# Up projection of a hybrid DiT layer: operands from fp32r pairs to scaled fp16 pairs, sizes from a second read of the weights, and a new order of products

## The chip, the core and the metric

The kernel runs on one core of a Trainium2 chip. The metric is device time in microseconds of one execution; the median of three runs is given.

## The reference

One layer of a diffusion transformer over 1024 latent tokens of width 1024 with 256 context tokens: a modulated RMS norm, one input projection that feeds a bidirectional chunkwise mLSTM and a windowed attention, two branch projections with sigmoid gates, an output projection, and a convolutional feed-forward part. The change touches the feed-forward part, cut to this:

```
x = x_mid + g2[:, None, :] * conv_ffn(modulate(rms_norm(x_mid, norm2_w[l]), sh2, sc2),
                                      w_up[l], conv_w[l], conv_b[l], w_down[l])

def conv_ffn(h, w_up, conv_w, conv_b, w_down):
    u = h @ w_up                                  # (1024, 1024) @ (1024, 5632)
    up = jnp.pad(u, ((0, 0), (r, r), (0, 0)))
    acc = conv_b
    for j in range(CONV_W):                       # width 3 along the tokens
        acc = acc + up[:, j:j + L] * conv_w[j]
    a, g = jnp.split(acc, 2, axis=-1)
    return (jax.nn.silu(g) * a) @ w_down
```

## The kernel before, in words

Products are kept near fp32 accuracy by splitting each operand into a high and a low half and adding three products (high x high, high x low, low x high): `product` (line 2021) issues three matmuls for each of four blocks of the inner dimension, each a 128x128 weight tile against 512 columns. `split_from` (line 50) makes the halves: ACT copies the high half (line 47), DVE subtracts it from the source for the low half (line 54; with a scale, line 56). Before the change the halves of the feed-forward part are fp32r, four bytes each; in the input projection they are fp16.

The tail (`stage_tail`) runs in stages. *Branch products* (960 to 1113 us): `branch("a")` and then `branch("m")`, seven products each by a Strassen-Winograd scheme, operand by operand from a queue (`operands`, i from 0 to 13 in each branch); sigmoid gates load on the ACT queue (line 1760). *Output projection* (1113 to 1208 us): `project` in two halves; then rows are normed (`square`, lines 1869 to 1874, with GpSimd's power), transposed and split into the activations' seven operands (`put`): b11, b21, t1 to t4, b22. *Unit stage* (1208 to 1645 us): the up projection in 22 units. A unit is one pair of 128 columns of `w_up` for the value half and the gate half, and again a Strassen-Winograd scheme: seven products with weight operands r1 (two products), q1 (two), q2 (two) and r2 (one), 7 x 4 x 3 = 84 matmuls. `lead` loads a unit's megabyte of weights on the SP queue and splits r1; `prep` and `prep2` make sums of the weight quarters (s12, s34) and split q1, q2, r2. `first_mm` runs the b11 product into bank pa and the b21 product into bank pc, `first_ev` empties them into the tile ua, `rest` does the other five into pa and pb, with an eviction (ACT copy or DVE addition) after each. `conv_gate` applies the convolution (one ACT operation, two DVE ones of three operands, for each half), the silu, the gate's product, and stores the result. In the same units DVE also makes sums of the down projection's weights (`weight_sums`), and later of the hidden rows (`hidden_sums`). *Down projection* (1645 us to the end): seven products again; while it runs, the last modulation rows (`last_row`, lines 2306 and 2308; tiles u4) are summed on DVE, and `mod_row` (line 288) adds each over the partitions by small fp32 matmuls.

A scheduler orders each engine's instructions from this program order. Each engine runs its own list in order, and an instruction waits for its operands and for its output's buffer. Pools hand out tiles: `x512` pools 0 to 6 hold eight tiles of 128x512 f32 each, `op4` ten of 128x1024, `op2` four of 128x512, `raw` two megabyte tiles, `accp` eight of 128x1024.

Of the kernel before, what the change touches and what calls it, by code (L numbers as in the profile page):

```python
# [18 lines left out]
P = 128  # L19
# [1583 lines left out]
def stage_tail(E, st):  # L1603
# [52 lines left out]

    g1b = tp1.tile([P, D], F32, name="g1b")
# [91 lines left out]

    def branch(nm, sg_d, pool):  # L1750
# [85 lines left out]
    def norm_factors():  # L1836

        nc.vector.scalar_tensor_tensor(m2[:, 1], m2[:, 1], 1.0, vecT[:, V_N2 : V_N2 + KT], op0=ALU.add, op1=ALU.mult)
        nc.vector.tensor_scalar(m2[:, 1], m2[:, 1], float(D) ** 0.5, None, op0=ALU.mult)

    sM.close()

# [7 lines left out]
    xj = tp1.tile([P, 640], F32, name="xj")[:, :512]  # L1850
# [33 lines left out]
    def put(m, k, src, s=slice(0, 512)):  # L1884
        if B.setdefault(m, [None] * H)[k] is None:
            B[m][k] = [x512(f"{m}{x}{k}", pool=homes[m]) for x in "hl"]
# [50 lines left out]
    def weight_sums(k, a0, a1, b0, b1, eng=None):  # L1937
# [11 lines left out]
        nc, lambda j: A["w_up"][j], lambda n: rawp.tile([P, KT, 256], F32, tag="raw", name=n), op4, op2,  # L1949
# [14 lines left out]
    norm_factors()  # L1964
    with tc.issue_after(held.ins):
# [18 lines left out]
    U.prep_apart(0, lambda n, dt=F32R: x512(n, dt, 1))  # L1984
# [34 lines left out]
    E.__dict__.update(xm_d=xm_d, g2b=g2b, T=T, weight_sums=weight_sums, sA=sA, sX=sX, x512=x512, rawp=rawp, op4=op4, op2=op2, accp=accp, U=U)  # L2019
# [12 lines left out]
class Units:  # L2032
# [3 lines left out]
    def __init__(self, nc, src, raw, op4, op2, bank, out, B):  # L2036
        self.nc, self.src, self.raw, self.op4, self.op2, self.bank, self.out, self.B = nc, src, raw, op4, op2, bank, out, B
# [15 lines left out]
    def lead(self, j):  # L2053
        self.raws[j] = raw = self.raw(f"ur{j}")
        self.nc.sync.dma_start(raw, self.src(j))
        if j != 2:
            self.R1[j] = self.pair(j, "r1", self.op4, raw[:, :, 0:P])

    def lead_first(self, j):
# [3 lines left out]
        self.R1[j] = self.pair(j, "r1", self.op4, raw)  # L2063
# [20 lines left out]
    def prep(self, j):  # L2084
# [6 lines left out]
        self.Q[j] = [self.pair(j, "q1", self.op4, s12)]  # L2091

    def prep2(self, j):
# [5 lines left out]
        self.Q[j] += [self.pair(j, "q2", self.op4, s34), self.pair(j, "r2", self.op2, a22)]  # L2099

    def prep_apart(self, j, new):
# [3 lines left out]
        s1, s2, s3, s4 = [self.v(new(f"s{i}_{j}", F32)) for i in range(1, 5)]  # L2105
# [4 lines left out]
        self.Q[j] = [sum([self.pair(j, f"q1{i}", new, s) for i, s in enumerate((s1, s2))], [])]  # L2110
# [338 lines left out]
```

## Time and profile before

| | |
|---|---|
| median of 3 runs | 1845.76 us (1845.05 to 1845.76) |
| profiled execution | 1849.14 us, span 1847.4 us |
| branch products | 960 to 1113 us |
| output projection, transposes | 1113 to 1208 us |
| unit stage | 1208 to 1645 us |
| down projection | 1645 to 1847 us |
| one unit in the middle | 19.04 us |

A row of the timeline reads: start, duration, engine, line, operation, out <- in by the program's names, shape. Matmuls are pipelined, so the pace of TensorE is read from start to start and not from durations; the same holds for the busy times of DVE and ACT, whose operations overlap by about 0.1 us. A row of windows gives the busy time and the number of instructions of each engine, the granted clock of TensorE, the share of the DMA engines and GB/s. `x8` on an fp32 matmul counts the passes that were recorded together.

### The profile page before, as it was taken

To read this page: it belongs to the slowest core of one execution; us is meant where nothing else is said; L and a number is where in the kernel's file an instruction comes from. 1 tells how busy PE (TensorE), PEld (TensorE's weight loads), DVE (VectorE), ACT (ScalarE), POOL (GpSimd) and SP (SyncE) were. 2 spreads that over 40 slices of the span, in tenths; PEclk is the share of its full clock that TensorE was granted. 3 is DMA by queue.
4 is the path that set the end of the run, shared out by engine and by line. 5 is a ranking of instruction groups with operands and counts; after the bars stand their busy time and mean duration, and the time that the engine had idled before them with its cause. 6 is when DMAs were issued, how large, how long until landed. Compare 5 with 4: busy or idle time off the path is not lost.

```text
span 1847.4 us, 27864 instructions
## 1 busy us (share of the span) xinstructions
PE 1790.8 (97%) x9207; PEld 1283.5 (69%) x9207; DVE 1425.9 (77%) x2864; ACT 1069.8 (58%) x2229; POOL 508.3 (28%) x747
## 2 busy tenths in 40 slices
PE   7989999999998899999999999999999999999999
PEld 3855555555554566656668887878888888888887
DVE  3858888888788686858687787698889898897665
ACT  4747877878787565645356462476444444465441
POOL 2467769587862530303010020000000000000000
PEclk9999999999999899999999999999999999999999
DMA  9747988888796625261359927322454544599751
GB/s 342 233 138 146 201 170 179 192 180 199 147 182 131 219 79 192 79 213 37 132 188 368 344 92 246 141 77 106 172 207 180 194 160 166 195 318 371 260 172 69
DMA packets 302193, 342.47 MB, mean 185 GB/s; under 512 B 176208, under 2 KB 200672, under 8 KB 299232
## 3 DMA queue, kind: packets, MB, share of 16 engines
q1 hardware_dynamic: 287648, 314.47, 56.3%
q10 hardware_dynamic: 14400, 26.22, 4.2%
q8 instruction: 72, 1.18, 0.3%
q14 instruction: 73, 0.60, 0.1%
HBM read 224.61 MB, written 76.16 MB: 163 GB/s over the span
## 4 chain that ended last, share of the span: by engine, by line
PE 78%; DVE 7%; DMA 4%; issue 3%; ACT 3%; POOL 3%; SPq 0%; ACTq 0%; DVEq 0%; POOLq 0%
PE g L706 8%; PE pq L706 6%; PE pa L2027 4%; PE pa L2029 4%; PE pa L2028 4%; PE po L706 3%; PE dx L2029 2%; PE dx L2027 2%; PE dx L2028 2%; PE pb L2027 2%; PE pb L2029 2%; PE pb L2028 2%; PE yb L2029 2%; PE yb L2027 2%; PE yb L2028 2%
## 5 line engine op out<-in xcount | busy, mean ns | idle before, releaser
L850 DVE CUSTOM_DVE_ANT_0 s<-s,maskA,nsink 128x640 f32<-128x640 f32 (+1 forms) x128 | 117.4, 917 | 65.5 <-PE s L845 65.0
L866 DVE TENSOR_TENSOR P<-s,P 128x640 f16<-128x640 f32 (+1 forms) x128 | 100.6, 786 | 1.0 <-ACT s L861 1.0
L860 ACT ACTIVATE P<-s,st 128x640 f16<-128x640 f32 (+1 forms) x128 | 98.2, 767 | 4.1
L706 PE MATMUL g<-hH,fh 128*128 128x512 f16 x256 | 97.1, 379 | 0.0
L706 PE MATMUL g<-hH,fl 128*128 128x512 f16 x256 | 97.0, 379 | 0.0
L706 PE MATMUL g<-hL,fh 128*128 128x512 f16 x256 | 97.0, 379 | 0.0
L861 ACT ACTIVATE s<-s,st 128x640 f32<-128x640 f32 (+1 forms) x128 | 93.8, 733 | 0.0
L706 PEld LDWEIGHTS <-hH 128*128 128x128 f16 x640 | 62.8, 99 | 37.3 <-issue 1.8
L858 ACT ACTIVATE st<-st,shift 128x1 f32<-128x1 f32 x128 | 37.6, 294 | 85.6 <-DVE st L850 84.8
L706 PE MATMUL pq<-wha,hH 128*128 128x384 f16 (+1 forms) x256 | 84.9, 332 | 0.1
L706 PE MATMUL pq<-wha,hL 128*128 128x384 f16 (+1 forms) x256 | 84.9, 332 | 0.0
L706 PE MATMUL pq<-wla,hH 128*128 128x384 f16 (+1 forms) x256 | 84.9, 332 | 0.0
L706 PEld LDWEIGHTS <-fh 128*128 128x128 f16 x512 | 49.2, 100 | 45.4
L2165 ACT ACTIVATE cv<-ua,vecT 128x1024 f32<-128x1024 f32 x22 | 27.4, 1246 | 84.9 <-DVE ua L2138 84.9
L1436 POOL TENSOR_SCALAR kwh<-k,gcall 128x128 fp32r<-128x128 f32 x72 | 32.5, 455 | 157.2 <-PE dC L164 53.9
L47 ACT ACTIVATE dfh<-drf 128x512 fp32r<-128x512 f32 x55 | 34.4, 628 | 59.3 <-PE dx L2028 26.5
L2027 PE MATMUL dx<-dwh,dfh 128*128 128x512 f32 (+1 forms) x176 | 68.3, 388 | 0.0
L2029 PE MATMUL dx<-dwh,dfl 128*128 128x512 f32 (+1 forms) x176 | 68.2, 388 | 0.0
L2028 PE MATMUL dx<-dwl,dfh 128*128 128x512 f32 (+1 forms) x176 | 68.2, 387 | 0.0
L54 DVE TENSOR_TENSOR dfl<-drf,dfh 128x512 fp32r<-128x512 f32 x55 | 37.6, 688 | 36.1 <-ACT dfh L47 36.1
L165 PE MATMUL kv<-whkv,hL 128*128 128x384 f16 x192 | 62.6, 326 | 0.0
L164 PE MATMUL kv<-wlkv,hH 128*128 128x384 f16 x192 | 62.6, 326 | 0.0
(691 smaller groups left out, 6249.9 us busy)
## 6 DMA issues: line engine op xcount, KB each, us to landing
ur<-in_w_up SPq DMA_DIRECT2D x22, 1024.0 KB
wmb<-in_w_modB SPq DMA_DIRECT2D x48, 256.0 KB
f_d<-cv SPq DMA_DIRECT2D x22, 512.0 KB
wm<-in_w_modA SPq DMA_DIRECT2D x16, 512.0 KB
fr<-in_w_g SPq DMA_DIRECT2D x32, 256.0 KB
drf<-fs_d SPq DMA_DIRECT2D x15, 512.0 KB
drw<-wt_d SPq DMA_DIRECT2D x14, 512.0 KB
w1b<-in_w_cx SPq DMA_DIRECT2D x16, 388.0 KB
```

The source lines that it names most:

```text
L54: rest = nc.vector.tensor_tensor(lo, src, whole, op=ALU.subtract)
L164: nc.tensor.matmul(ps, lh[:, ls], rl[:, rs], start=False, stop=False)
L165: nc.tensor.matmul(ps, ll[:, ls], rh[:, rs], start=False, stop=stop and i == n - 1)
L706: nc.tensor.matmul(self.ps, x, w, start=self.i == 0, stop=self.i == self.n - 1)
L850: nc.vector.tensor_tensor_reduce(e, e, self.mask, scale=self.ss[:, h : h + 1], scalar=nsink[:, hh : hh + 1], op0=ALU.add, op1=ALU.min, acc ...
L858: nc.scalar.activation(m, st4[:, 8 + h : 9 + h], AF.Identity, bias=shift)
L860: nc.scalar.activation(two[:, :W], e, AF.Exp, bias=m, scale=-1.0)
L861: nc.scalar.activation(e, e, AF.Exp, bias=m, scale=-1.0, accum_out=st4[:, 4 + h : 5 + h])
L866: nc.vector.tensor_tensor(two[:, W : 2 * W], self.e[h], two[:, :W], op=ALU.subtract)
L2027: nc.tensor.matmul(ps, lh, rh, start=start and i == 0, stop=False, skip_group_check=True)
L2028: nc.tensor.matmul(ps, lh, rl, start=False, stop=False, skip_group_check=True)
L2029: nc.tensor.matmul(ps, ll, rh, start=False, stop=stop and i == n - 1, skip_group_check=True)
```

## The change

Four things change together.

1. Every operand of the up projection is an fp16 pair: high and low half lie in one tile of the size of one former half. The weights are multiplied by a factor of their unit as they are split, so the split's DVE part becomes a three-operand instruction. The activations are scaled by one factor (`xbound`), worked into the norm's scale and shift.
2. A unit's factor is a power of the sum of the squares of its weights. The weights are read a second time for it, in four pieces of 256 KB (`size_load`): for units 0 to 3 on the ACT queue during the branch products, for the others on the SP queue four units ahead. ACT squares each piece with a sum along the row (`measure`); `measured` adds the four columns over the partitions by four fp32 matmuls with a matrix of ones (bank ub), then one DVE operation, a power on GpSimd, a reciprocal on DVE, and two GpSimd operations that put the inverse factors into the convolution's weights.
3. From unit 2 on, the next unit's first two products stand inside a unit: b11 between t1 and t3, b21 between b22 and t4. `prep` and `prep2` of the next unit are issued inside the unit, the sizes of the third unit ahead are added up just before t4, and r1 is split two units ahead.
4. The weights of a unit are fetched one unit earlier (`fetch(j + 3)`).

```diff
+    def measure(j, i, raw):
+        if i == 0:
+            F[j] = tp1.tile([P, 16], F32, tag="uf", name=f"uf{j}", bufs=8)
+        w = E.junk[:, : raw.shape[1]] if raw.shape[1] <= E.junk.shape[1] else raw
+        nc.scalar.activation(w, raw, AF.Square, accum_out=F[j][:, i : i + 1])
+    def size_load(pool, j, k, queue):
+        um = pool(f"um{j}{k}")
+        queue.dma_start(um.rearrange("p (k c) -> p k c", k=2), A["w_up"][j][:, 2 * k : 2 * k + 2])
+        UM.append((j, k, um))
+    def ahead_sizes(n):
+        if 6 <= n < 22:
+            size_load(lambda nm: up.tile([P, 512], F32, tag="um", name=nm), (n - 6) // 4, (n - 6) % 4, nc.scalar)
+        if 8 <= n < 24:
+            measure(*UM.pop(0))
...
             for i in (2 * p, 2 * p + 1):
+                ahead_sizes(i if nm == "a" else 14 + i)
...
+        q = tp1.tile([P, 24], F32, name="xbound")
+        nc.gpsimd.tensor_tensor(q[:, 8:16], m2[:, 1], m2[:, 1], op=ALU.mult)
+        nc.scalar.activation(q[:, 16:24], q[:, 8:16], AF.Square, accum_out=q[:, 0:1])
+        nc.scalar.activation(q[:, 16:24], m2[:, 0], AF.Square, accum_out=q[:, 1:2])
+        nc.tensor.matmul(pb[:, 0:2], E.ones, q[:, 0:2], start=True, stop=True)
...
+        nc.gpsimd.tensor_scalar(m2, m2, xs_[:, 0:1], None, op0=ALU.mult)
+    def measured(j, n):
+        f = F[j]
+        pb = tp_tile(f"ub{j}")
+        for i in range(n):
+            nc.tensor.matmul(pb[:, 0:1], E.ones, f[:, i : i + 1], start=i == 0, stop=i == n - 1)
+        nc.vector.tensor_scalar(f[:, 4:5], pb[:, 0:1], 2.0 ** -26, 1e-36, op0=ALU.mult, op1=ALU.add)
+        nc.gpsimd.tensor_tensor(f[:, 5:6], f[:, 4:5], expo[:, 0:1], op=ALU.pow)
+        nc.vector.reciprocal(f[:, 6:7], f[:, 5:6])
+        nc.gpsimd.tensor_scalar(f[:, 7:8], f[:, 6:7], xs_[:, 1:2], None, op0=ALU.mult)
+        nc.gpsimd.tensor_scalar(f[:, 8:14].rearrange("p (i u) -> p i u", i=3), cw, f[:, 7:8], None, op0=ALU.mult)
...
     def pair(self, j, nm, new, src):
-        p = self.v(new(f"{nm}h{j}")), self.v(new(f"{nm}l{j}"))
-        split_from(self.nc, *p, src)
+        p = [self.v(t) for t in new(f"{nm}{j}")]
+        split_from(self.nc, *p, src, scale=self.F[j][:, 5:6])
...
         product(nc, pb, op(q1, 0), B["t1"], True)
         copy_act(nc, ug[:, t1], pb)
+        between(0)
+        if new is not None:
+            r1 = self.R1.pop(new)
+            na, un = self.bank("A", f"pa{new}"), self.out("u", f"ua{new}")
+            product(nc, na, self.op(r1, 0), B["b11"], True)
+            copy_act(nc, un[:, t0], na)
         product(nc, pa, op(q2, 0), B["t3"], False)
         nc.vector.tensor_tensor(ug[:, t1], pa, ug[:, t1], op=ALU.add)
+        between(1)
         product(nc, pb, op(q2, 4), B["b22"], False)
         nc.vector.tensor_tensor(ua[:, t1], pb, ua[:, t1], op=ALU.add)
+        if new is not None:
+            pc = self.bank("C", f"pc{new}")
+            product(nc, pc, self.op(r1, 4), B["b21"], True)
+            nc.vector.tensor_tensor(un[:, t0], pc, un[:, t0], op=ALU.add)
+            self.mid[new] = na, un
+        between(2)
         product(nc, pa, op(r2, 0), B["t4"], False)
...
+    def between(j):
+        def part(i):
+            n = j + 2
+            if 2 <= j < NFC - 1 and i < 2:
+                (U.prep, U.prep2)[i](j + 1)
+            if 4 <= n + 1 < NFC and i == 2:
+                E.measured(n + 1, 4)
+        return part
...
+        elif j + 2 < NFC:
+            U.lead(j + 2)
+        if 1 <= j < NFC - 3:
+            U.fetch(j + 3)
+        if 4 <= j + 4 < NFC:
+            for k in range(4):
+                E.size_load(lambda nm: E.x512(nm, F32, 4), j + 4, k, nc.sync)
         sums(j - 1, a)
         a = conv_gate(j, *u)
+        while E.UM:
+            E.measure(*E.UM.pop(0))
```

How the order of instructions moves is shown at three places. First TensorE before, at the end of unit 14 and the start of unit 15 (pa14 is the unit's bank, t4h and t4l the halves of the activations' operand, r2 and r1 the weights'):

```order
L2027 MATMUL pa14_16660<-t4h3_14757,r2h14_16636 128x512
L2028 MATMUL pa14_16660<-t4l3_14758,r2h14_16636 128x512
L2029 MATMUL pa14_16660<-t4h3_14757,r2l14_16637 128x512
L2027 MATMUL pa15_16800<-b11h0_14285,r1h15_16758 128x512
L2028 MATMUL pa15_16800<-b11l0_14286,r1h15_16758 128x512
L2029 MATMUL pa15_16800<-b11h0_14285,r1l15_16759 128x512
```

After, the same engine just ahead of unit 14's t4 (both halves now bear one name; ub17 is the bank of unit 17's sizes, uf17 its columns):

```order
L2095 MATMUL pc15_17114<-b213_14510,r115_16992 128x512
L2096 LDWEIGHTS r115_16992
L2096 MATMUL pc15_17114<-b213_14510,r115_16992 128x512
L2097 LDWEIGHTS r115_16992
L2097 MATMUL pc15_17114<-b213_14510,r115_16992 128x512
L1897 MATMUL ub17_17128<-uf17_17025,ones_106 128x1 x4
L2095 LDWEIGHTS r214_16939
L2095 MATMUL pa14_16905<-t40_14825,r214_16939 128x512
```

The next unit's b21 product (pc15) and the four sizing matmuls of unit 17 now stand ahead of unit 14's t4, and weight loads are instructions of their own.

Second VectorE in the same unit, before (cv are the convolution's tiles, q1l, q2l and r1l the low halves):

```order
L2167 SCALAR_TENSOR_TENSOR cv14_36_16793<-ug14_16690,vecT_68,cv14_36_16793 128x1023
L2077 TENSOR_TENSOR ua15_16826<-pc15_16801,ua15_16826 128x512
L54 TENSOR_TENSOR q1l16_16906<-s12_16_16902,q1h16_16905 128x1024
L2171 TENSOR_TENSOR cv14_14_16789<-cv14_14_16789,cv14_36_16793 128x1024
L2097 TENSOR_TENSOR s34_16_16909<-ur16_16896 128x512
```

and after:

```order
L2250 SCALAR_TENSOR_TENSOR cv14_14_17173<-ua14_16906,uf14_16543,cv14_14_17173 128x1023
L2219 TENSOR_TENSOR ua15_17065<-pc15_17114,ua15_17065 128x512
L1898 TENSOR_SCALAR uf17_17025<-ub17_17128 128x1
L2251 SCALAR_TENSOR_TENSOR cv14_14_17173<-ua14_16906,uf14_16543,cv14_14_17173 128x1023
L1900 RECIPROCAL uf17_17025<-uf17_17025 128x1
L2162 TENSOR_TENSOR s12_17_17376<-ur17_17154 128x512
L56 SCALAR_TENSOR_TENSOR r117_17310<-ur17_17154,uf17_17025,r117_17310 128x1024
```

The size's two one-column operations stand between the eviction and the sums, with one convolution operation between them, and the splits take the factor uf17 as a third operand.

Third ScalarE at the start of the branch products, before (baw and baa are the weights and the activations of branch a):

```order
L47 ACTIVATE bawh1_0_12181<-bawr1_12179 128x512
L47 ACTIVATE baah2_0_12227<-baar2_12225 128x512
L47 ACTIVATE bawh1_1_12183<-bawr1_12179 128x512
L47 ACTIVATE baah3_0_12279<-baar3_12277 128x512
L47 ACTIVATE baah2_1_12229<-baar2_12225 128x512
L47 ACTIVATE baah1_0_12201<-baar1_12199 128x512
```

and after (um01 is the second piece of unit 0's sizes, xj a scratch tile):

```order
L47 ACTIVATE bawh1_0_12181<-bawr1_12179 128x512
L47 ACTIVATE baah2_0_12231<-baar2_12229 128x512
L1772 ACTIVATE xj_12220,uf0_12673<-um00_12555 128x512
L47 ACTIVATE bawh1_1_12183<-bawr1_12179 128x512
L47 ACTIVATE baah2_1_12233<-baar2_12229 128x512
L47 ACTIVATE baah1_0_12201<-baar1_12199 128x512
L47 ACTIVATE bawh2_0_12241<-bawr2_12239 128x512
L47 ACTIVATE baah1_1_12203<-baar1_12199 128x512
L47 ACTIVATE baah3_0_12283<-baar3_12281 128x512
L1772 ACTIVATE xj_12220,uf0_12673<-um01_12621 128x512
L1778 DMA um10_12794<-in_w_up 128x512
L1772 ACTIVATE xj_12220,uf0_12673<-um02_12671 128x512
```

The square of unit 0's first piece now stands behind the first two splits of the branch, and two more squares and an issue of a load behind the next six.

Two things move without being named in the diff. Eight of the sixteen `last_row` sums (tiles u4_0 and their loads) stand in the unit stage, since the tiles of x512 pool 3 are free earlier. Six squares of units 5 and 6 (um50 to um61) stand on ACT ahead of the q11 split of unit 1.

More of the change, by code (lines that the diff above doesn't have):

```diff
@@ L1885, in put @@
         if B.setdefault(m, [None] * H)[k] is None:
-            B[m][k] = [x512(f"{m}{x}{k}", pool=homes[m]) for x in "hl"]
+            B[m][k] = xpair(f"{m}{k}", homes[m])
         split_from(nc, *[o[:, s] for o in B[m][k]], src)
@@ L1964, in stage_tail @@
     norm_factors()
+    for j in range(4):
+        measured(j, 4)
     with tc.issue_after(held.ins):
@@ L2018, in stage_tail @@
         put("t4", k, raw0(k + H))
-    E.__dict__.update(xm_d=xm_d, g2b=g2b, T=T, weight_sums=weight_sums, sA=sA, sX=sX, x512=x512, rawp=rawp, op4=op4, op2=op2, accp=accp, U=U)
+    E.__dict__.update(xm_d=xm_d, g2b=g2b, T=T, weight_sums=weight_sums, sA=sA, sX=sX, x512=x512, rawp=rawp, op4=op4, op2=op2, accp=accp, U=U, measure=measure, measured=measured, size_load=size_load, UM=UM)
     stage_ffn(E, st)
```

90 lines of the change are left out of this document (58 added, 32 removed).

## The prediction

> **What bounds the kernel now.** I read the page first: its busy line, then the chain that ended last.
>
> ```profile
> span 1847.4 us, 27864 instructions
> PE 1790.8 (97%) x9207; PEld 1283.5 (69%) x9207; DVE 1425.9 (77%) x2864; ACT 1069.8 (58%) x2229; POOL 508.3 (28%) x747
> PE 78%; DVE 7%; DMA 4%; issue 3%; ACT 3%; POOL 3%; SPq 0%; ACTq 0%; DVEq 0%; POOLq 0%
> ```
>
> TensorE sets the time; the other engines matter where they make it wait. Second, the windows, for the stages that the change touches (columns: busy time and instructions of PE, PEld, DVE, ACT, POOL; granted clock; DMA share; GB/s).
>
> ```profile
> 960.00:990.00 30.00, 29.07 (x127) 23.32 (x126) 23.23 (x39) 15.59 (x30) 0.00 (x0) 1.00 1.01 378
> 990.00:1020.00 30.00, 30.00 (x134) 24.86 (x133) 25.59 (x43) 22.24 (x42) 0.00 (x0) 1.00 1.01 359
> 1050.00:1080.00 30.00, 30.00 (x134) 24.86 (x133) 24.62 (x37) 19.91 (x38) 5.77 (x4) 1.00 0.57 193
> 1208.00:1300.73 92.73, 91.11 (x406) 74.12 (x405) 86.34 (x133) 58.38 (x96) 2.47 (x1) 1.00 0.26 91
> 1300.73:1319.77 19.04, 19.04 (x85) 15.77 (x84) 16.89 (x20) 9.03 (x12) 0.00 (x0) 1.00 0.51 193
> 1605.37:1624.41 19.04, 19.04 (x85) 15.77 (x84) 16.05 (x21) 11.37 (x19) 0.00 (x0) 1.00 0.91 330
> ```
>
> The last two rows are one unit of the up projection each: 84 matmuls in 19.04 us, no gap, full clock. So a unit is 84 x 226.7 ns and nothing else, and DVE has 2.15 us to spare in it, ACT 10. The front of the stage (1208 to 1300.7) is tighter: PE idles only 1.62 us there, but DVE is busy 93%. The branch products, where the first sizes are now loaded, have DMA engines that are full until 1050 and yet no PE gap after 990.
>
> **The change part by part.** *fp16 halves.* The number of matmuls stays; each takes the pace of an fp16 stream. Here are the first and the last of 48 fp16 matmuls of that shape (timeline of TensorE):
>
> ```profile
> 944.60 0.39 PE L163 MATMUL mo<-hH,whqo 128*128 128x512 f16 x1
> 954.75 0.38 PE L165 MATMUL mo<-hH,wlqo 128*128 128x512 f16 x1
> ```
>
> 10.15 us / 47 = 216 ns, against 19.04 / 84 = 226.7. Saved: 10.7 ns x 84 = 0.90 us per unit, x 22 = **-19.7 us**, as far as TensorE stays the bound.
>
> *Sizing matmuls.* Each unit gets four fp32 matmuls of a 128x128 matrix of ones against one column. The kernel has this form already, in the row products of the modulation (an fp16 neighbourhood first, then the down projection's f32 one):
>
> ```profile
> 323.64 0.95 PE L288 MATMUL ms<-expo,macc 128*128 128x1 f32 x8
> 324.45 0.32 PE L842 MATMUL s<-KA,QT 128*128 128x384 f16 x1
> ...
> 1713.72 0.95 PE L288 MATMUL dy<-expo,u 128*128 128x1 f32 x8
> 1714.53 0.49 PE L2027 MATMUL dx<-dwh,dfh 128*128 128x512 f32 x1
> 1714.86 0.39 PE L2028 MATMUL dx<-dwl,dfh 128*128 128x512 f32 x1
> ```
>
> Four matmuls are eight passes and hold the stream 0.81 us; behind them the f32 neighbour needs 0.33 to the next start instead of 0.227, so 0.91 there. They stand inside the stream, just ahead of t4, and nothing can run beside them on PE. Eighteen units x 0.81 = 14.6; the four of units 0 to 3 stand in the f32 output projection: 4 x 0.91 = 3.6; the two-column product of the activations' scale about 0.3 (an estimate, a third of that). **+18.5 us.** The upper bound is 0.91 for all, +20.3; the lower is the case in which short passes hide under the long stream, 0, and I know no row that shows it. A unit becomes 84 x 0.216 + 0.81 = 18.95 us. The page "FP8 and Floating Point Precision" of the Trainium skill (section TensorE Precision Notes) says that a true fp32 product takes four passes through the array; by it the block would be sixteen passes and twice as long. The row shows x8 for four matmuls, so the trace does not agree, and I keep 0.81.
>
> *DVE in a unit.* It gives its time by pitch, start to start (timeline of VectorE):
>
> ```profile
> 1311.90 1.28 DVE L2166 SCALAR_TENSOR_TENSOR cv<-ug,vecT,cv 128x1023 f32<-128x1023 f32 x1
> 1313.09 0.69 DVE L1906 TENSOR_TENSOR wb<-wb 128x512 f32<-128x512 f32 x1
> 1313.70 1.28 DVE L2167 SCALAR_TENSOR_TENSOR cv<-ug,vecT,cv 128x1023 f32<-128x1023 f32 x1
> 1314.89 0.69 DVE L2077 TENSOR_TENSOR ua<-pc,ua 128x512 f32<-128x512 f32 x1
> 1315.49 1.22 DVE L54 TENSOR_TENSOR q1l<-s,q1h 128x1024 fp32r<-128x1024 f32 x1
> 1316.62 1.22 DVE L2171 TENSOR_TENSOR cv<-cv,cv 128x1024 f32<-128x1024 f32 x1
> ```
>
> 1.19 for the three-operand form, 0.60 and 1.13 for two operands. Before: 4 x 1.19 + 12 x 0.60 + 4 x 1.13 = 16.5. The scaled splits are three-operand (+0.06 on each of three long ones and on the short one: +0.24), and the two one-column operations add about 0.25: 17.0. New waits: the reciprocal stands one long operation behind the sum it needs, with GpSimd's power in between. That power has a normal and a bad size:
>
> ```profile
> 1211.69 2.47 POOL L1874 TENSOR_TENSOR rrx<-rrx,expo 128x1 f32<-128x1 f32 x1 [7.88 <-DVE rrx L1873]
> L1874 POOL TENSOR_TENSOR rrx<-rrx,expo 128x1 f32<-128x1 f32 x8 | 6.3, 792 | 93.6 <-DVE rrx L1873 93.6
> ```
>
> (6.3 - 2.47) / 7 = 0.55 us in seven cases, 2.47 in the one that ran beside two-operand work of DVE. I take about 1 us of waiting per unit, so DVE needs 18 of 18.95: **0**, and it is the thinnest cover of the change. The moved products leave evictions more room, since pa and pb are now written again after 24 matmuls (24 x 0.216 = 5.2 us) instead of 12.
>
> *ACT.* Squares cost, by pitch (timeline of ScalarE):
>
> ```profile
> 1210.18 0.63 ACT L1870 ACTIVATE xj<-acc 128x512 f32<-128x512 f32 x1 [0.59 <-DVE acc L1861]
> 1210.72 0.19 ACT L1870 ACTIVATION_READ_ACCUMULATOR xj<-acc 128x1 f32 x1
> 1210.82 0.40 ACT L47 ACTIVATE t1h<-acc 128x256 fp32r<-128x256 f32 x1
> ```
>
> 0.64 each, four per unit = 2.6 us; ACT goes from 9.0 to 11.6 of 18.95. Hidden: **0** in the steady units.
>
> *The second read.* 22 MB. In a steady unit the measured 193 GB/s has room for one more MB (+55). Four MB fall into the branch products, mostly while the DMA engines are full: 3 MB / 370 GB/s is 8 us of transfer at worst. PE shows 30.00 of 30 there, and the share falls to 0.57 after 1050, so operands lead by enough; between 0 and +8, I take **+0.5**. SP's queue passes, per unit, a fetch one unit earlier and four small loads; their buffers are free a unit ahead, and the stores behind them have no reader within the unit: 0.
>
> *Start of the branch products.* Here ACT feeds PE directly, and the measures of unit 0 stand between its splits (order of ScalarE).
>
> ```profile
> 959.54 0.50 PE L2027 MATMUL yb<-baah,bawh 128*128 128x512 f32 x1 [2.48 <-ACT bawh L47]
> 960.73 0.50 PE L2027 MATMUL yb<-baah,bawh 128*128 128x512 f32 x1 [0.46 <-DVE mo L1534]
> 962.60 0.96 PE L2029 MATMUL yb<-baah,bawl 128*128 128x512 f32 x3 [0.47 <-DVE bawl L54]
> 958.51 0.33 ACTq L1760 DMA_DIRECT2D sga<-sga_d  x1
> ```
>
> One measure stands ahead of all but the first two splits, two issues of sizes (0.33 each) and three more measures follow. The first product is paced by ACT for some 4 us; one measure is 0.64, all four and two issues 3.2. Between 0.6 and 3.2: **+1**. If a measure's load is late, ACT waits with all splits behind it (rival C).
>
> *Front of the units.* DVE is 93% busy, and here it gets the scale and size operations, the scaled splits, the waits on GpSimd, and 8 rows of the modulation sum that the order moves forward out of the down projection, since their buffers come free earlier:
>
> ```profile
> L2308 DVE SCALAR_TENSOR_TENSOR u<-u,sil,u 128x512 f32<-128x512 f32 x14 | 10.5, 747 | 2.0 <-DMA u<-in_w_modB 2.0
> ```
>
> 8 x 0.75 = 6.0 for the rows and 3 x 1.5 for the first three units (0.5 of work and 1.0 of waits, as above), 10.5 in all. PE wants 3 x 0.9 = 2.7 less there and DVE had 92.73 - 86.34 = 6.4 of idle time: upper bound 10.5 + 2.7 - 6.4 = +6.8. Lower bound -1.6, PE's idle time there. Some of the rows stand in later units with spare time, so **+2**, nearer to the lower end.
>
> Sum: -19.7 + 18.5 + 0.5 + 1 + 2 = +2.3. The profiled execution takes 1849.14 (its span and 1.74), which is 3.38 above the median of the runs; it would be 1851.4, and the median 1845.76 + 2.3 = **1848.0**.
>
> **The rivals.**
> *A. The sizes are cheap.* If the short passes hide, the 18.5 goes: 1829.5; at half of their price 1838.8. For it: PE's weight loads are overlapped everywhere else. Against it: both rows of L288 show the full 0.81. The same side is reached, just, if every stall lies at its low end: -1.2 net of PE (-19.7 + 18.5), -1.6 in the front and about -1 of the waits at the branch's start give 1842. Together 0.18.
> *B. DVE becomes the bound of a unit.* Place: the reciprocal between the two convolution operations, and GpSimd's two scalings behind it. Price: a power of 2.47 leaves 2.47 - 1.19 = 1.3 us of wait, the two scalings beside three-operand work may hold DVE about 0.5 each: 17.0 + 1.3 + 1.0 = 19.3, with a wait for the split's high half (0.2) 19.5; 18 units x 0.55 = +10, so 1858. It decides from the point at which DVE's unit passes 18.95. The page "SBUF — State Buffer" (section Who interferes with whom) states that a DVE instruction with two SBUF inputs contends with a GpSimd instruction that reads SBUF; the row of 2.47 agrees, and whether DVE too is held no row shows. Chance 0.15.
> *C. ACT waits in order for sizes.* Place: the first splits of branch a, and the q11 split of unit 1, which stands behind six measures whose buffers the measures before them free. Price: one round trip of a transfer at its worst row below, 4.8, once or twice less the cover of two units: +4 to +8, 1852 to 1856. Chance 0.2.
>
> ```profile
> 1210.17 4.77 DMA xm_d<-acc
> ```
>
> *D. The pace does not come,* because fp16 weights are loaded by instructions of their own. Then +19.7 and 1868. Against it: the quoted fp16 products load weights the same way. Chance 0.02.
>
> **How the numbers follow.** The forecast has 0.45; A 0.18, B, C and D 0.37. About 0.2%, 3.7 us, is what a measurement of this kernel can tell from no change; the forecast's own range is taken as that band, 1842.1 to 1849.4. Leaving out D, half of A and the far end of B, the range is 1841 to 1858. Faster 0.18, same 0.45, slower 0.37.
>
> **What would show it.** In the profile after: matmuls of pa and pb at 216 ns; a block of x8 on ub holding PE 0.81 us; steady units of 18.95 us with no other gap; a branch start about 1 us longer. The forecast is wrong if a unit is 18.3 or less (A), if PE waits for DVE in steady units (B), or if ACT idles on a size load while PE waits for a split (C).

## The result and the profile after

The changed kernel takes 1890.22 us (median of 4 runs, 1888.58 to 1891.88) against 1845.66 us (also of 4 runs): 1.0241 times as long, interval 1.0224 to 1.0257. The forecast was 1848.0, with a range from 1841 to 1858. The page after:

```profile
span 1889.2 us, 28670 instructions
PE 1802.5 (95%) x9385; PEld 1142.1 (60%) x9385; DVE 1436.4 (76%) x2910; ACT 1134.8 (60%) x2409; POOL 589.0 (31%) x820
PE 51%; DVE 21%; DMA 12%; ACT 6%; issue 5%; POOL 4%; SPq 1%; ACTq 0%; DVEq 0%; POOLq 0%
```

TensorE is still busy 95%, yet its share of the chain fell from 78% to 51%, and DVE and DMA took it over. The windows tell where. A stage is cut at its first matmul, the output projection also at the first transpose behind it; by this the units before end at 1632.10, and not at 1645. First the kernel before, for the branch products, the output projection, the units and the down projection:

```profile
959.50:1113.70 154.20, 153.23 (x673) 126.07 (x674) 123.38 (x190) 94.28 (x174) 17.92 (x12) 1.00 0.73 265
1113.70:1186.30 72.60, 71.84 (x314) 58.23 (x313) 51.25 (x76) 19.88 (x38) 2.76 (x5) 1.00 0.64 232
1208.50:1632.10 423.60, 421.98 (x1865) 348.09 (x1864) 378.86 (x486) 219.77 (x297) 2.47 (x1) 1.00 0.46 170
1632.10:1847.40 215.30, 211.68 (x951) 175.61 (x949) 143.27 (x229) 83.07 (x145) 0.00 (x0) 1.00 0.65 231
```

The same four of the kernel after:

```profile
957.50:1123.40 165.90, 159.45 (x673) 129.97 (x673) 124.17 (x190) 105.16 (x209) 18.09 (x12) 0.95 0.73 265
1123.40:1204.70 81.30, 79.01 (x348) 64.54 (x347) 53.70 (x87) 21.18 (x39) 10.84 (x23) 0.96 0.58 207
1226.90:1673.70 446.80, 423.31 (x2010) 199.61 (x2009) 395.16 (x533) 272.60 (x442) 74.94 (x55) 0.99 0.62 211
1673.70:1889.20 215.50, 211.87 (x952) 175.81 (x950) 135.47 (x216) 82.07 (x140) 0.00 (x0) 1.00 0.61 210
```

The spans differ by 41.8 us: the branch products begin 2.0 earlier and take 11.7 more, the output projection 8.7 more, the units 23.2, the down projection 0.2; the transposes between (22.2 us) are the same. (Over the traces of all kernels here the branch products begin anywhere from 952.8 to 959.5, so the 2.0 is not shown to be the change's.) In the first two stages TensorE is *busy* longer with nearly the same matmuls, at a granted clock of 0.95 and 0.96: part of the loss is slow clock.

The units hold the forecast's own sum where nothing disturbs them. A sizing block of TensorE, and two units from sizing block to sizing block (timeline, then windows):

```profile
1331.91 0.95 PE L1897 MATMUL ub<-uf,ones 128*128 128x1 f32 x8
1332.72 0.38 PE L2095 MATMUL pa<-t,r 128*128 128x512 f16 x1
```

```profile
1331.91:1350.85 18.94, 18.94 (x94) 9.09 (x93) 18.49 (x25) 11.70 (x20) 4.53 (x3) 1.00 0.77 263
1391.74:1415.48 23.74, 20.78 (x93) 9.55 (x92) 18.18 (x24) 12.59 (x20) 4.36 (x3) 0.93 0.69 231
```

18.94 us was forecast as 18.95, the block as 0.81. The second unit is 4.8 us longer, 2.96 of it a gap and the rest slow clock (0.93). What TensorE waits for in the stage of units (waits of PE; total, times, longest):

```profile
PE pa L2095 <- ACT ug L47: 14.0, 12, 3.0
PE pb L2095 <- ACT ug L47: 5.2, 5, 1.5
PE pa L2095 <- ACT ua L47: 2.1, 3, 1.0
```

It waits for evictions, which are copies by ScalarE, an engine that is busy 61% there. The gap of 2.96 shows why (timelines of DVE, POOL, ACT and PE):

```profile
1396.23 0.69 DVE L1972 TENSOR_TENSOR wa<-wa 128x512 f32<-128x512 f32 x1 [3.57 <-DMA wa<-in_w_dn]
1399.95 0.15 DVE L1898 TENSOR_SCALAR uf<-ub 128x1 f32<-128x1 f32 x1
1400.25 0.86 POOL L1899 TENSOR_TENSOR uf<-uf,expo 128x1 f32<-128x1 f32 x1 [17.30 <-DVE uf L1898]
1401.15 1.76 ACT L47 ACTIVATE r<-ur,uf 128x1024 f16<-128x1024 f32 x2 [7.21 <-POOL uf L1899]
1402.81 0.58 ACT L47 ACTIVATE ug<-pa 128x512 f32<-128x512 f32 x1
1403.44 0.38 PE L2095 MATMUL pa<-b,r 128*128 128x512 f16 x1 [2.96 <-ACT ug L47]
```

Read it upwards: PE waits for the copy of ug; the copy stands on ScalarE behind the splits r of a later unit; these have waited 7.21 us for their factor; the power waited for DVE's small operation on ub; and that stood on DVE behind weight sums that had waited for a transfer. No engine is full. Queues in order tie a bank's eviction to a factor that nobody needs yet.

### The profile page after: what moved, and what is told of

It reads as the page before. It is cut to its first block, busy times and chain, and to the rows that moved or that the text cites. A ratio compares the mean times of both kernels' runs of the same rounds, so it can differ in the third digit from the quotient of the medians.

```text
span 1889.2 us, 28670 instructions
## 1 busy us (share of the span) xinstructions
PE 1802.5 (95%) x9385; PEld 1142.1 (60%) x9385; DVE 1436.4 (76%) x2910; ACT 1134.8 (60%) x2409; POOL 589.0 (31%) x820
## 4 chain that ended last, share of the span: by engine, by line
PE 51%; DVE 21%; DMA 12%; ACT 6%; issue 5%; POOL 4%; SPq 1%; ACTq 0%; DVEq 0%; POOLq 0%
PE g L706 8%; PE pq L706 6%; PE po L706 3%; PE dx L2095 2%; PE dx L2097 2%; DVE cv L2250 2%; PE dx L2096 2%; DMA wb<-in_w_dn 2%; DVE cv L2251 2%; PE dy L2097 2%; PE dy L2096 2%; PE dy L2095 2%; DVE r L56 1%; PE mo L165 1%; PE mo L163 1%
## 5 line engine op out<-in xcount | busy, mean ns | idle before, releaser
L850 DVE CUSTOM_DVE_ANT_0 s<-s,maskA,nsink 128x640 f32<-128x640 f32 (+1 forms) x128 | 117.4, 918 | 63.9 <-PE s L845 63.4
L1899 POOL TENSOR_TENSOR uf<-uf,expo 128x1 f32<-128x1 f32 x22 | 22.6, 1031 | 316.5 <-DVE uf L1898 316.5
L47 ACT ACTIVATE r<-ur,uf 128x512 f16<-128x512 f32 (+1 forms) x43 | 38.4, 924 | 67.6 <-POOL uf L1899 63.0
L2095 PE MATMUL pa<-t,q 128*128 128x512 f16 x176 | 66.7, 379 | 2.2 <-ACT ua L47 2.1
```

The source lines that it names most:

```text
L47: return nc.scalar.activation(out, in_, AF.Copy, scale=scale)
L850: nc.vector.tensor_tensor_reduce(e, e, self.mask, scale=self.ss[:, h : h + 1], scalar=nsink[:, hh : hh + 1], op0=ALU.add, op1=ALU.min, acc ...
L2095: nc.tensor.matmul(ps, lh, rh, start=start and i == 0, stop=False, skip_group_check=True)
```

## The experiments

Three theories were put up. **Q**, the queue: ScalarE waits for factors with evictions behind. **D**, the transfers: the second read delays other loads. **V**, VectorE: it has too much work for a unit. The table gives each kernel's median, its ratio to the kernel before as measured in the same session, with the interval, and the lengths of the three stages in its one trace. A stage also varies by itself: the output projection takes 76.9 to 81.3 us in changed, e1, e6, e10 and e11, whose work there is the same, so a few us of one stage in one trace say little.

| kernel | median us | ratio (interval) | branch | output | units |
|---|---|---|---|---|---|
| before | 1845.7 | | 154.2 | 72.6 | 423.6 |
| changed | 1890.2 | 1.0241 (1.0224 to 1.0257) | 165.9 | 81.3 | 446.8 |
| e1 r1 behind eviction | 1871.1 | 1.0134 (1.0113 to 1.0155) | 164.4 | 77.0 | 432.4 |
| e2 constant factor | 1832.2 | 0.9925 (0.9905 to 0.9945) | 154.9 | 72.6 | 409.6 |
| e3 no second read | 1870.8 | 1.0138 (1.0115 to 1.0161) | 154.2 | 76.6 | 439.3 |
| e5 one sizing matmul | 1879.3 | 1.0179 (1.0163 to 1.0195) | 163.7 | 78.2 | 442.5 |
| e6 r1 a unit earlier | 1874.9 | 1.0153 (1.0136 to 1.0170) | 165.2 | 76.9 | 436.6 |
| e7 = e6 + e5 | 1877.4 | 1.0166 (1.0151 to 1.0182) | 164.2 | 78.0 | 441.4 |
| e8 = e7 + late sizes | 1873.8 | 1.0146 (1.0129 to 1.0164) | 168.8 | 73.9 | 440.3 |
| e9 = e2, old order | 1842.0 | 0.9981 (0.9971 to 0.9992) | 154.0 | 72.7 | 419.4 |
| e10 r1 and r2 behind | 1864.1 | 1.0103 (1.0073 to 1.0133) | 166.3 | 78.9 | 423.4 |
| e11 work kept, wait cut | 1872.1 | 1.0142 (1.0124 to 1.0160) | 166.5 | 80.4 | 434.3 |
| e13 = e11 + e3 | 1853.2 | 1.0040 (1.0027 to 1.0053) | 154.8 | 81.2 | 424.9 |
| e14 = e10 + e5 + late sizes | 1859.0 | 1.0080 (1.0067 to 1.0094) | 169.7 | 75.4 | 424.0 |
| e16 = e10 + e5 | 1858.5 | 1.0080 (1.0063 to 1.0097) | 163.9 | 78.4 | 423.9 |
| e15 = e16, less DVE work | 1845.1 | 1.0004 (0.9990 to 1.0018) | 164.1 | 77.6 | 409.5 |

**e1.** One edge in the order:

```diff
-        copy_act(nc, ug[:, t0], pa)
+        self.last = copy_act(nc, ug[:, t0], pa)
...
-            U.lead(j + 2)
+            with tc.issue_after(U.last.ins):
+                U.lead(j + 2)
```

> The changed kernel with one edge more in the order: the split of r1 for the unit two ahead stands on ScalarE behind the copy that empties t4's bank, instead of ahead of it. Theory Q (ScalarE's queue): in the units PE waits for that copy because the split ahead of it waits for its unit's factor (GpSimd's power, behind VectorE's late TENSOR_SCALAR). Then the 14.0 us of waits of pa and 5.2 of pb for ug, and the slow clock behind them, mostly go: 15 to 25 us less than the changed kernel's 1890, 1865 to 1875. Theory D (the second read's transfers delay the loads that VectorE waits for): no order of ScalarE helps, 1885 to 1892. Theory V (VectorE has too much work for a unit of 18.95 us): the wait only moves to another eviction, over 1883.

1871.1, inside Q's band; the units lost 14.4 us by an edge that changes no work and no transfer. A new wait of TensorE for r1's low half appeared (7.3 us), since the split had moved by more than a unit.

**e2.** The factors become a constant, and the second read, its squares and the sizing matmuls go with them (shown in part):

```diff
...
-        for i in range(n):
-            nc.tensor.matmul(pb[:, 0:1], E.ones, f[:, i : i + 1], start=i == 0, stop=i == n - 1)
-        nc.vector.tensor_scalar(f[:, 4:5], pb[:, 0:1], 2.0 ** -26, 1e-36, op0=ALU.mult, op1=ALU.add)
-        nc.gpsimd.tensor_tensor(f[:, 5:6], f[:, 4:5], expo[:, 0:1], op=ALU.pow)
-        nc.vector.reciprocal(f[:, 6:7], f[:, 5:6])
+        nc.gpsimd.memset(f[:, 5:6], 2.0 ** 9)
+        nc.gpsimd.memset(f[:, 6:7], 2.0 ** -9)
```

> fp16 halves, scaled splits and the new order of products stay; the factors are a constant (2 to the 9th), so there is no second read, no square, no sizing matmul of the units and no wait for a factor (the activations' scale stays). Left out: the factors are not computed from the weights. My sum for the fp16 pace is -19.7 us on 1845.7. Theories Q and D: 1824 to 1830, since both costs go with the sizes. Theory V: the scaled splits and the new order alone keep VectorE late, over 1835.

1832.2, between the bands: faster than before by 0.75%, but the units take 409.6 and not 423.6 - 19.7 = 403.9.

```profile
1204.90:1614.50 409.60, 402.84 (x1865) 182.31 (x1865) 388.48 (x495) 226.70 (x298) 48.71 (x57) 1.00 0.54 187
```

```profile
PE pa L2088 <- DVE ug L2205: 3.7, 7, 1.2
```

(The window of the units, then the largest of TensorE's waits in them.) DVE is busy 388 of 410 us, and the largest wait is for one of its evictions. So without any sizes the faster pace already brings DVE close to being the bound.

**e3.** The squares read a resident matrix of ones:

```diff
-        um = pool(f"um{j}{k}")
-        queue.dma_start(um.rearrange("p (k c) -> p k c", k=2), A["w_up"][j][:, 2 * k : 2 * k + 2])
-        UM.append((j, k, um))
+        UM.append((j, k, E.ones))
...
-        nc.scalar.activation(w, raw, AF.Square, accum_out=F[j][:, i : i + 1])
+        nc.scalar.activation(w, raw[:, None, :].to_broadcast([P, 4, P]), AF.Square, scale=2.0 ** -5, accum_out=F[j][:, i : i + 1])
```

> Everything of the changed kernel but the transfers of the second read: the squares read a resident matrix of ones (with a scale that gives the same factor). Left out: the factors are not computed from the weights. Theory D: the late load ahead of branch m's split (5.4 + 1.0 us of gap and about 3.3 of slow clock) and the late loads of the weight sums in the units go, 1860 to 1870. Theory Q: the branch gets its 9.7 us back, the units keep most of their stalls, 1874 to 1882. Theory V: as Q.

1870.8, above D's band by a hair and below Q's: both are at work. The branch is back at 154.2 to the tenth, the units got 7.5 back, the output projection 4.7 (which e13 does not repeat). The transfers cost the branch its 11.7 us: kernels without the second read have a branch of 154.0 to 154.9 (e2, e3, e9, e13), all with it 163.7 to 169.7. In the units VectorE's waits for loads of weight sums fall from 14.3 to 7.5 us and TensorE's for ug from 19.2 to 11.4. ScalarE's wait for factors does not fall (63.6 us against 60.7), so how the transfers cost the units 7.5 us stays open. What they did to the branch in the changed kernel (ACT, then three rows of PE, then the window behind the gap):

```profile
1069.76 0.63 ACT L47 ACTIVATE bmwh<-bmwr 128x512 fp32r<-128x512 f32 x1 [4.24 <-DMA bmwr<-in_w_bm]
1075.19 0.80 PE L2095 MATMUL yb<-bmah,bmwh 128*128 128x512 f32 x1 [5.40 <-ACT bmwh L47]
1077.44 0.79 PE L2097 MATMUL yb<-bmah,bmwl 128*128 128x512 f32 x1 [1.03 <-DVE bmwl L54]
1083.16 0.48 PE L2095 MATMUL yb<-bmah,bmwh 128*128 128x512 f32 x1
```

```profile
1076.00:1083.00 7.00, 5.97 (x14) 4.40 (x14) 7.00 (x12) 6.73 (x14) 0.24 (x1) 0.50 0.55 157
```

A weight load comes 4.24 us late, ScalarE stops, TensorE stops 5.4 and 1.0 us, and then runs at a granted clock of 0.50 until 1083: 13 steps in 5.72 us instead of 13 x 0.227 = 2.95.

**e5.** One matmul with four columns, and their sum on DVE:

```diff
-        for i in range(n):
-            nc.tensor.matmul(pb[:, 0:1], E.ones, f[:, i : i + 1], start=i == 0, stop=i == n - 1)
-        nc.vector.tensor_scalar(f[:, 4:5], pb[:, 0:1], 2.0 ** -26, 1e-36, op0=ALU.mult, op1=ALU.add)
+        nc.tensor.matmul(pb[:, 0:n], E.ones, f[:, 0:n], start=True, stop=True)
+        nc.vector.reduce_sum(f[:, 4:5], pb[:, 0:n], axis=AX.X)
+        nc.vector.tensor_scalar(f[:, 4:5], f[:, 4:5], 2.0 ** -26, 1e-36, op0=ALU.mult, op1=ALU.add)
```

> The four sizing matmuls of a unit become one with four columns (two passes), and VectorE adds the four columns from PSUM in one more small operation. The forecast's price is 0.81 us for eight passes: two passes cost 0.2, so 22 x 0.6 = 13 us less on TensorE, 1877, if TensorE's own work sets the units. Theories Q and V: in the units that stall, the time comes from the waiting chain and the saving is swallowed in part: 1880 to 1888.

1879.3, just below the band of Q and V. The units gave 4.3 of 18 x 0.6 = 10.8 us: TensorE's own work did not set all of them.

**e6.** As e1, with `U.last` of the unit before, so that r1 stands directly behind the eviction.

> As the first experiment, but the split of r1 stands behind the eviction of t4 one unit earlier, directly behind it instead of directly ahead as in the changed kernel. In the first experiment the wait for ug fell by 16.6 us and a new one of 7.3 us for r1's low half appeared, since the split had moved by more than a unit. Theory Q: both waits go, 5 to 8 us below the first experiment's 1871, 1863 to 1867. Theory V: VectorE's backlog only shows at another place, 1869 to 1875.

1874.9, in V's band and no better than e1. By the numbers this spoke against Q. ScalarE's waits in the units of e6, however, show the same wait still there:

```profile
ACT r L47 <- POOL uf L1899: 46.5, 13, 6.1
```

All 13 of these are splits of 128x512, so r2's, each with the copy of ug next behind it; e1 has the same (51.2 us). The edge had moved half of the cause; e10 moves the other half.

**e7** joins e6 and e5.

> The previous one and a single sizing matmul of four columns per unit. With the queue's waits gone TensorE sets the units, so theory Q expects the whole 22 x 0.6 = 13 us that the single matmul alone did not bring (it brought 11, of which 4.3 in the units): 1850 to 1855. Theory V: VectorE has 18 us of work and waits in a unit of then 18.34 us, so most of it is swallowed: over 1858.

1877.4, no gain, as V expected; with the queue still in place it told nothing by itself.

**e8** loads the sizes of units 0 to 3 in branch m, two at each of its steps 6 to 13 (shown in part; the squares follow two steps later):

```diff
...
-        if 6 <= n < 22:
-            size_load(lambda nm: up.tile([P, 512], F32, tag="um", name=nm), (n - 6) // 4, (n - 6) % 4, nc.scalar)
+        if 20 <= n < 28:
+            with tc.issue_after(SPLIT["m", n - 14].ins):
+                for i in (2 * n - 40, 2 * n - 39):
+                    size_load(lambda nm: up.tile([P, 512], F32, tag="um", name=nm), i // 4, i % 4, nc.scalar)
```

> The previous one, and the sizes of units 0 to 3 are loaded in branch m behind its steps 6 to 13, when the DMA engines have room, instead of while they are full. Theory D for the branch: the late load ahead of a split, its gap and the slow clock behind it go, 9.7 us less than the previous kernel: 1840 to 1846. If the squares of late loads stop ScalarE near the end of branch m instead, no gain or a loss.

1873.8: a miss; the band had counted on e7 at 1850 to 1855. The late load's wait fell from 4.9 to 1.3 us, and in its place the two-column product for the activations' scale, now early on TensorE, waited for a bank:

```profile
PE xbound L1888 <- DVE sgm L1821: 7.7, 1, 7.7
```

**e9** is e2 with the old order of products and splits, and with it the old, later fetch of a unit's weights.

> Constant factors as in the second experiment, but the old order of products: the next unit's b11 and b21 stand behind t4 again and the splits of a unit are issued one unit ahead. Left out: the factors are not computed from the weights. If the new order is worth something with the fp16 pace (12 matmuls are 2.6 us of cover for an eviction, 24 are 5.2), it is slower than the second experiment's 1832: 1835 to 1845. If the order gives nothing: 1828 to 1833.

1842.0 against 1832.2: the new order, with the earlier fetch, is worth 9.8 us with fp16, all of it in the units (419.4 against 409.6). The wait that the old order leaves is for the copy of ua, 12 matmuls after its bank was filled:

```profile
PE pa L2088 <- ACT ua L47: 7.6, 13, 1.8
```

**e10** is e6 with r2's split behind the eviction as well:

```diff
-        self.Q[j] += [self.pair(j, "q2", self.pair4, s34), self.pair(j, "r2", self.pair2, a22)]
+        q2 = self.pair(j, "q2", self.pair4, s34)
+        with self.tc.issue_after(self.last.ins) if j > 2 else nullcontext():
+            self.Q[j] += [q2, self.pair(j, "r2", self.pair2, a22)]
```

> In the sixth experiment's trace ScalarE still waits 46.5 us for factors, with another split of the same unit (r2, of 512 columns) now ahead of the evictions: only half of the queue had been moved. Here r1 and r2 both stand behind the eviction of t4. Theory Q: the stage of units, 436.6 us there, falls to 420 to 426 and the whole to 1860 to 1866. Theory V (VectorE's work and its waits for ScalarE's convolution set the unit): 1870 to 1876, as in the two before.

1864.1 and units of 423.4, both inside Q's bands. The window of the units and ScalarE's wait for factors there:

```profile
1225.40:1648.80 423.40, 417.87 (x2009) 199.22 (x2009) 395.19 (x532) 273.20 (x443) 67.45 (x55) 1.00 0.65 222
```

```profile
ACT r L47 <- POOL uf L1899: 2.5, 4, 0.8
```

60.7 us of waiting for factors became 2.5, the clock is 1.00, and 23.4 us went, with every load, square and matmul still there. Theory Q is shown for the units: by pace and sizes alone they would take 423.6 - 19.7 + 14.6 = 418.5, the changed kernel takes 28.3 more, and two edges take back all but 4.9 of it.

**e11** keeps the work and cuts the wait: the splits read a constant, and so do the inverse factors (shown in part).

```diff
...
-        split_from(self.nc, *p, src, scale=self.F[j][:, 5:6])
+        split_from(self.nc, *p, src, scale=self.K[:, 0:1])
```

> The changed kernel with all its work (loads, squares, sizing matmuls, power, reciprocal, scalings), but the splits and the inverse factors read a constant, so no split waits for a factor. Left out: the factors are not computed from the weights. Theory Q: the units lose the stalls that hang on the factor, about 15 to 20 of the 446.8 us, and the branch and the output projection stay as they are: 1869 to 1876. Theory V: 1883 to 1891, since VectorE's and GpSimd's work is the same. Theory D: 1885 or more, the loads are all there.

1872.1, in Q's band, but the units are 434.3 and not e10's 423.4: 12.5 us less instead of the 15 to 20 expected. The order is the scheduler's own again, PE waits 7.7 us for ua in six places, and ScalarE's splits now wait for VectorE's sums s of the unit's weight quarters:

```profile
ACT q L47 <- DVE s L2175: 43.2, 14, 5.8
```

With 10.4 for the other sum that is 53.6 us, against 19.3 in the changed kernel. The factor is one thing that a split can wait for ahead of an eviction. e10's edges put two of the splits behind the eviction whatever they wait for.

**e13** is e11 without the second read.

> The previous one, with squares of the resident ones instead of the second read (as in the third experiment). What is left of the change beside the fp16 pace and the order is TensorE's sizing matmuls and the small operations. If Q and D together are the whole loss beyond the forecast's sum: branch and output projection as in the third experiment (-9.7 and -4.7), the units 418 to 426: 1848 to 1857. Theory V: over 1860.

1853.2, within the band. The units met it (424.9), 9.4 below e11: the transfers cost the units something that does not go through the factor. The output projection did not (81.2 instead of 76.6), so its loss is not the transfers'. In the changed kernel it is made of this (PE twice, then the window):

```profile
1173.94 1.05 PE L1897 MATMUL ub<-uf,ones 128*128 128x1 f32 x8 [1.55 <-DVE xbound L1884]
1177.29 0.77 PE L164 MATMUL op<-wo1l,yh 128*128 128x512 f32 x1
```

```profile
1175.00:1180.00 5.00, 5.00 (x18) 4.24 (x19) 0.83 (x7) 2.56 (x4) 4.47 (x13) 0.55 0.44 185
```

The small products cost about 4 us, one of them waits 1.55 for a bank that DVE empties late, and slow clock follows (0.96 over the stage, some 3.3 us). In e1, e3 and e6 the stage has the same products at a clock of 1.00 and takes 76.6 to 77.0. With the sizes gone (e2), it is at 72.6 again.

**e14** puts e10, e5 and e8 together, with the scale and the first four sizes pinned into the output projection.

> A version that computes the factors and keeps every part of the change, with the causes taken away one by one: r1 and r2 behind the eviction of t4 (experiment ten), one sizing matmul of four columns (five), the sizes of units 0 to 3 loaded late in branch m (eight), and the scale of the activations and these four sizes pinned behind the fourth tile of the output projection, so that the two-column product no longer waits on TensorE for a bank as in the eighth experiment (7.7 us). Theory Q and D: units 423.4 - 22 x 0.6 = 410 to 414 us, branch 154 to 158, output projection to the transposes 75 to 78: 1838 to 1846, at or below the kernel before. If the late loads only move the wait within the branch, 1848 to 1854.

1859.0: above the 1838 to 1846 hoped for, and beyond the 1854 of the milder failure. The units stayed at 424, and a new wait stood at the end of the branch. The split it waits for stands on ScalarE behind late squares and behind waits for GpSimd; their shares were not taken apart:

```profile
PE op L163 <- ACT wo0h L47: 11.2, 1, 11.2
```

**e16** is e10 and e5 alone; **e15** is e16 without VectorE's sums for the down projection in the units:

```diff
+        if k < E.w_early:
-        sub(a0, a1, a0)
-        sub(a1, b1, a1)
-        sub(b1, b1, a0)
-        sub(b0, b0, b1)
+            sub(a0, a1, a0)
+            sub(a1, b1, a1)
+            sub(b1, b1, a0)
+            sub(b0, b0, b1)
```

(and the four sums of the hidden rows likewise, so e15 does not compute the layer).

> Experiment ten (both splits behind the eviction) and one sizing matmul of four columns per unit, with the sizes loaded early as in the changed kernel. Theory Q alone: TensorE sets the units once the queue's wait is gone, and 22 x 0.6 = 13 us come off: units 411 to 414, in all 1849 to 1853. Theory V as the floor beneath Q: VectorE has 395 us of work in the 423 of experiment ten and its own waits, the units stay at 420 to 425: 1859 to 1865, with the gain only in the output projection.

> The previous one without VectorE's sums for the down projection inside the units (four operations of 0.6 us in 19 units; the loads and stores stay). Left out: the sums of the down projection's weights from the fourth on and of the hidden rows, so the output is wrong. Theory V as the floor: VectorE's 2.4 us per unit less let TensorE set the units, 18 x 18.3 us and the front: 405 to 412, in all 1843 to 1850. If TensorE or the queue and not VectorE holds the previous one: within 4 us of it.

1858.5, a hair below V's band with the units inside it, and 1845.1; the windows of the units, e16 first:

```profile
1217.30:1641.20 423.90, 409.94 (x1902) 188.32 (x1901) 394.86 (x550) 272.42 (x443) 86.45 (x55) 0.99 0.65 223
```

```profile
1219.50:1629.00 409.50, 405.70 (x1902) 186.98 (x1901) 354.05 (x482) 274.30 (x443) 78.20 (x55) 1.00 0.67 231
```

In e16 TensorE's busy time fell by 8 us against e10 and the stage by nothing. TensorE's longest waits in its units:

```profile
PE pa L2096 <- DVE ug L2215: 5.8, 7, 1.4
PE pb L2096 <- ACT ug L47: 4.4, 2, 3.4
PE pa L2096 <- ACT ua L47: 2.5, 1, 2.5
```

Counted at every 84th matmul of pa, pb and pc, twelve of the eighteen units from the fourth to the last but one take 18.1 to 18.3 us, TensorE's own pace with the cheaper matmul. The other six take 18.6 to 19.8: there TensorE waits for VectorE's eviction. The rest of the gain is lost at the ends, behind copies by ScalarE: the first three units take 64.6 us (62.8 in e10) and the last 23.8 (19.5). In e15 DVE's busy time fell by 41 us and the stage by 14.4; the waits for VectorE's eviction are gone, and every unit from the fourth to the last but one takes 18.2 to 18.3. So VectorE is the next floor in some of the units, as V has it, but not in all. Which part of it holds them is not shown: e15 takes away the sums together with their waits for loads, and ScalarE's wait for factors falls with them, from 24.8 us to 8.5.

Of the versions that keep the whole computation, none beats the kernel before: e16 and e14 come nearest at 1.0080. e2 beats both, for weights to which its constant fits.

## Why the prediction was wrong

- *fp16 pace, -19.7 us: right.* Eleven steps in the middle of a unit take 2.37 us, 215.5 ns each, against 216:

```profile
1505.22 0.38 PE L2095 MATMUL pa<-b,r 128*128 128x512 f16 x1 [0.41 <-ACT ug L47]
1507.59 0.38 PE L2097 MATMUL pa<-b,r 128*128 128x512 f16 x1
```

- *Sizing matmuls, +18.5 us: right in the units (14.6 of it),* 0.81 each there, and 18.94 for a unit. The row shows x8 for four matmuls again, so two passes each, against the page "FP8 and Floating Point Precision" of the Trainium skill (section TensorE Precision Notes), which gives a true fp32 product four.
- *"ACT goes from 9.0 to 11.6 of 18.95. Hidden: 0": this is the step that failed.* The sum of busy times was right (11.70 in the window above); the term left out was the wait. The change gives ScalarE's splits a third input, and the prediction named the new wait on VectorE (the reciprocal) but not the one on ScalarE (the split itself), nor what stands behind the split: in the rows of the gap the copy of ug follows right behind r. Putting r1 and r2 behind the eviction was worth 23.4 us (e10); taking the wait for the factor away and leaving the order to the scheduler was worth 12.5 (e11).
- *The second read, +0.5, between 0 and +8: mis-sized.* Without it the branch is 11.7 us shorter (e3), more than the upper end. Some 10.2 of this stand at the late load, which is paid twice, as a gap (5.4 and 1.0) and as slow clock behind it. The "30.00 of 30" of before showed that there was no gap, not how near one was. "0" for the steady units was wrong too: without the loads the units lose 7.5 us (e3), and 9.4 where no split waits for a factor (e13 against e11).
- *Start of the branch products, +1: not contradicted.* The first 168 matmuls of the stage take 41.4 us against 39.9 before, +1.5 and inside the stated 0.6 to 3.2. But e2 and e9, which have no early squares, take 40.6 and 39.8, so at most a part of it is shown to be theirs.
- *Output projection, 3.9 us: right for the small products* (76.6 to 77.0 in e1, e3 and e6 against 72.6). The changed kernel lost 8.7, with a wait of 1.55 and slow clock that were not in the sum.
- *Front of the units, +2: a little low.* The first three units take 63.9 us against 61.8 before. Less 2.7 for the pace and with 1.6 for two sizing blocks 60.7 were due, so the front cost 3.2 (in e10 2.9 by the same count, with one block), inside the stated -1.6 to +6.8.
- *Rival B* was right that VectorE comes next (e16, e15), but this was not what slowed the changed kernel. *Rival C* had the right engine and the right form, a queue in order that waits ahead of what TensorE needs, but looked for a size's load where a split waited for a factor. *Rival A* is out by the sizing block of 0.81, *rival D* by the pace of 215.5 ns.

## What to carry to other kernels

When a change gives an instruction a new input, follow that input back through every queue, and list what stands behind the instruction on its own engine: an engine that is busy 61% can stop TensorE if an eviction stands behind a split whose factor nobody needs yet. Here two edges that pin such splits behind the eviction changed no work and brought 23 us of the units back. When the first wait is gone, ask at once what is next: here VectorE's late evictions and copies at both ends of the stage swallowed the gain of the cheaper matmul.

## What the runs showed of the hardware

Slow clock followed some short gaps and not others. After 1.44 us without work, and 1.03 us five microseconds before, the pace halved for a while (timeline of PE in the first units; 1274.54 is the first matmul at full pace again):

```profile
1270.27 0.38 PE L2095 MATMUL pb<-b,q 128*128 128x512 f16 x1 [1.44 <-ACT ug L47]
1271.59 0.63 PE L2097 MATMUL pb<-b,q 128*128 128x512 f16 x1
1272.02 0.63 PE L2095 MATMUL pb<-b,q 128*128 128x512 f16 x1
...
1274.54 0.38 PE L2095 MATMUL pa<-t,r 128*128 128x512 f16 x1
```

0.43 us from start to start instead of 0.216, from about 1271 to 1274.5, so some 1.7 us lost. The page "TensorE: Matmul & The Clock Gate" of the Trainium skill (section HAM oscillation) puts the danger at idle gaps of more than about 3.4 us; here slow clock also came behind 1.44 us, and behind the 1.55 in the output projection. Yet these two gaps of the same trace were longer, and for six us behind each the granted clock was 1.00:

```profile
1381.39 0.38 PE L2095 MATMUL pa<-b,r 128*128 128x512 f16 x1 [1.60 <-ACT ug L47]
1464.09 0.38 PE L2095 MATMUL pa<-b,r 128*128 128x512 f16 x1 [1.61 <-ACT ug L47]
```

So the length of a gap alone did not decide, and what did is not shown. Where slow clock followed, a wait cost more than its length: 1.7 us in the first rows above and nearly 3 behind the gap in branch m.

GpSimd's small operations took longer beside VectorE's work, and VectorE's did not. In the units a scaling and the power took this long (groups of POOL); in the output projection, with VectorE idle, a scaling took 0.30 us and a power 0.57. VectorE's three-operand instruction beside one of them kept its time:

```profile
L1901 POOL TENSOR_SCALAR uf<-uf,xscale 128x1 f32<-128x1 f32 x18 | 30.0, 1667 | 5.3 <-DVE uf L1900 5.3
L1899 POOL TENSOR_TENSOR uf<-uf,expo 128x1 f32<-128x1 f32 x18 | 20.4, 1135 | 316.5 <-DVE uf L1898 316.5
```

```profile
1401.41 1.78 POOL L1901 TENSOR_SCALAR uf<-uf,xscale 128x1 f32<-128x1 f32 x1 [0.30 <-DVE uf L1900]
1401.23 1.26 DVE L2251 SCALAR_TENSOR_TENSOR cv<-ua,uf,cv 128x1023 f32<-128x1023 f32 x1
```

It took 1.28 us before, and in the changed kernel 1.27 on average in 30 cases beside these operations and 1.28 in 54 others. Rival B's term of 0.5 us for holding VectorE is not seen. The prediction tied the slow power of 2.47 us to two-operand work of VectorE; three of its seven cases of 0.55 overlapped such work too, for 0.3 to 0.4 us, so that work alone does not make a power slow.
